# Two experts per token: rows of their own in memory in place of adding scatters into one row

## The chip, the cores and the metric

The kernel runs on one core of a Trainium2 chip. The metric is device time in microseconds (us), the median of several executions. A difference is called real here from 2% on.

## What is computed

The program is one layer of a decoder trunk for 512 tokens of width 1024. After a token mixer (state space, pooling, attention) with its residual comes a hierarchical mixture of 16 experts: each token picks one group of four experts and the two best experts in it, and their outputs are added to the residual with weights. A final norm ends it. Cut to what matters here:

```python
x = x + concat(A, B, C) @ w_out                 # x2 below: the residual of the second half
h = rms_norm(x, norm2_g)
# comb[t, e]: weight of expert e for token t; two of the 16 are not zero
act = silu(h @ w_gate[e]) * (h @ w_up[e]) * comb[:, e]
x = x + sum over e of act @ w_down[e]
out = rms_norm(x, final_norm_g)
```

## The kernel before

**Order of the work.** Streams of steps (Python generators such as `s_gate_up`, `s_down`, `y_out`, `s_meta`, `s_last`) are emitted in the order in which a planner (`Flow`) estimates that their engines would start them. A step names its engine, the events that it needs (`fl.sig`, `fl.sig_dma`) and the tokens that it takes. Each engine then runs its instructions in that fixed order and waits on semaphores. If an estimate changes, the order of everything behind it can change.

**Experts.** Each expert has 96 slots. The tokens' normed rows are scattered by GpSimd into `x_scr` (`scatter`), one slot for each of a token's two experts, and read back transposed as `xts`. The weights (fp32, 3 MB per expert) come through a ring of five staging buffers `stg` of 512 KB each. ScalarE writes the high fp16 half of each staged part, VectorE the low half (`gu`, `dn`), which frees the staging buffer. An expert is then 24 products for gate and up (`pg`), silu on ScalarE and a product on VectorE (`xs`), two transposes (`pta`), the split `aT`, and 12 products `py`. Experts overlap: TensorE does the products of one while the other engines finish the one before.

**Rows out (`y_out`).** VectorE scales the left half of an expert's 96 output rows into a buffer `ys`, ScalarE the right half. There are two such buffers. GpSimd then starts an indirect DMA that adds the rows to `acc_scr`, one row per token in device memory, which holds the residual x2 before (`s_acc`):

```python
pool.indirect_dma_start(
    out=acc_scr[:, :], out_offset=bass.IndirectOffsetOnAxis(ap=B["tok"][0:CAP, e:e + 1], axis=0),
    in_=ys[0:CAP, :], in_offset=None, compute_op=ALU.add)
```

All these DMAs write one tensor, and each waits for the one before. Unused slots point at spare rows behind the 512 tokens.

**The end.** The last expert (15) writes no rows to memory: TensorE multiplies its rows `ys` with a matrix of its tokens' places (`hot_e`) in `s_last`. Once the scatter of expert 14 has landed (`("y1", NE - 2)`), SP reads the four token tiles `xt` back from `acc_scr`. For tiles 0 and 1 VectorE adds the product to `xt`; for tiles 2 and 3 (`PADD`) TensorE adds `xt` by an fp32 product with the identity. Squares on ScalarE, a power on GpSimd and a scaling on VectorE end each tile, and SP stores it.

**Clears (`s_clear`).** SP writes zeros over `x_scr` (20 parts of 512 KB) and one part of `acc_scr` in the first quarter.

**Beyond the slots.** If an expert has more than 96 tokens, a dense pass at the end recomputes; it is behind a branch.

Of the kernel before, what the change touches and what calls it, by code (L numbers as in the profile page):

```python
# [9 lines left out]
F16 = mybir.dt.float16  # L10
# [9 lines left out]
P = 128  # L20
# [58 lines left out]
class _Engine:  # L79
    """An engine whose instructions also advance the flow's estimate of its time."""  # L80
# [16 lines left out]
class Flow:  # L97
    """Emits streams of instructions in the order in which their engines would start them.

    A stream is a generator. It yields (engine, needs, tokens) ahead of a step: the engine that the  # L100
    step starts on, events that other streams signal, and tokens to take. The step that could start
    first is emitted next; a lower rank goes first among equals.
    """
# [170 lines left out]
def hybrid_trunk_kernel(tc, a, out, cap=CAPACITY, dbg=None):  # L274
# [22 lines left out]
    m_scr = dram.tile([NSLOT + 2 * S, 2], F32, name="m_scr")  # L297
    acc_scr = dram.tile([S + P, D], F32, name="acc_scr")
# [9 lines left out]
    # Pages of 8 KB per partition, which change hands. Those of the experts' weights:  # L308
# [71 lines left out]
    def less_busy(margin):  # L380
        """Whether GpSimd is free so much earlier than VectorE."""
        return fl.free.get("dve", 0.0) > max(fl.t, fl.free.get("pool", 0.0)) + margin

# [28 lines left out]
    # weights of the dense layers and of the experts share one ring of staging buffers  # L412
# [140 lines left out]
    def s_prep():  # L553
# [26 lines left out]
        # (lambda_bar - 1) / lambda  # L580
# [28 lines left out]
    def s_prep_b():  # L609
        # chunk input map, transposed on the tensor engine  # L610
# [28 lines left out]
    def s_prep_e():  # L639
        # unit phases e^{i 8 theta c}, c = 0..63, and partners that invert them exactly  # L640
# [37 lines left out]
    def s_prep_c():  # L678
# [3 lines left out]
        # C lambda^tau, tau = 0..8 (imaginary part negated)  # L682
# [28 lines left out]
        # response within a chunk, laid out as a block Toeplitz matrix through DRAM  # L711
# [31 lines left out]
    def s_bias():  # L743
        # one row per query of a 64-query tile
# [31 lines left out]
    def s_clear():  # L776
        # rows of the routed tokens' buffer that no token takes read as zeros
        for r in range(0, NSLOT + 2 * S, P):
            yield "sp", ("zero", ("start", "k0"))
            sp.dma_start(x_scr[r:r + P, :].rearrange("p (j c) -> p j c", c=512),  # L780
                         zero.unsqueeze(1).to_broadcast([P, 4, 512]))
        yield "sp"
        sp.dma_start(acc_scr[S:S + P, :].rearrange("r (j c) -> r j c", c=256),
                     zero.bitcast(F32).unsqueeze(1).to_broadcast([P, 4, 256]))
        sp.dma_start(m_scr[0:NSLOT, :], a["meta0"])

# [415 lines left out]
    def s_norm2(m):  # L1202
        """x2 * norm2_g and its transpose for the router; 1 / rms comes in later."""
# [23 lines left out]
    pads = cst.tile([P, 4 * NT], F32, name="pads")  # L1227
    mt_ = cst.tile([P, NT, 2, 2], F32, name="mt_")
# [10 lines left out]
    def s_route(m):  # L1239
# [30 lines left out]
        # first of the largest groups, then the first two of its largest experts  # L1270
# [82 lines left out]
    def s_gather(m):  # L1353
        """The first expert's tokens, transposed: a product with the tokens' places, each part exact."""
# [21 lines left out]
    def s_gates():  # L1376
        """Gate weights, each with its token's number, and those of pairs beyond an expert's slots."""
# [6 lines left out]
        v.tensor_copy(mt_[:, :, :, 0], cpk[:, C_TOK:C_TOK + NT].unsqueeze(2).to_broadcast([P, NT, 2]))  # L1384
# [53 lines left out]
    def s_acc():  # L1438
        for m in range(NT):
            yield "sp", (("x2", m, 0), ("x2", m, 1))  # L1440
            sp.dma_start(acc_scr[m * P:(m + 1) * P, :], x2_t[m])
            fl.sig_dma(("acc", m))

# [1 line left out]
    we = {}  # L1445

    # When the places of the weights come free.
# [108 lines left out]
    def s_meta():  # L1556
        yield "pool", ("meta", "B")
        mt = B["ex"].tile([P, NE, 2], F32, tag="mt", name="mt", bufs=1)
# [8 lines left out]
        for t in range(NT):  # L1567
            yield "dve", (("dstart", 5),)
            if t == 0:
                B["hot"] = B["ex"].tile([P, S], F16, name="hot_e", bufs=1)  # L1570
            v.tensor_scalar(B["hot"][0:CAP, t * P:(t + 1) * P], cpk[0:CAP, C_COL:C_COL + P],
                            mt[0:CAP, NE - 1, 0:1], -float(t * P), ALU.subtract, ALU.is_equal)
# [5 lines left out]
        for t in range(NT):  # L1578
            yield "sp", (("y1", NE - 2),), ("stg",)
            xt[t] = stage.tile([P, D], F32, tag="stg", name=f"xt{t}")  # L1580
            sp.dma_start(xt[t], acc_scr[t * P:(t + 1) * P, :])
            fl.sig_dma(("xt", t))

    xt, yo = {}, {}
    PADD = (2, 3)               # tiles whose residual is added on TensorE
    ssz = cst.tile([P, NT, 3], F32, name="ssz")

    def s_last(ys):
        """The last expert's rows go to their tokens on TensorE, and the sum to SBUF."""
# [47 lines left out]

    def y_out(e, nh, py, ys):
# [19 lines left out]
        else:  # L1658
# [4 lines left out]
            pool.indirect_dma_start(  # L1663
                out=acc_scr[:, :], out_offset=bass.IndirectOffsetOnAxis(ap=B["tok"][0:CAP, e:e + 1], axis=0),
                in_=ys[0:CAP, :], in_offset=None, compute_op=ALU.add)
            fl.give("ys")
            fl.sig(("y1", e))

# [74 lines left out]
    rv = nc.values_load(flag[:1, :1], min_val=0, max_val=S)  # L1743
    with tc.If(rv > CAP):
        with tc.tile_pool(name="fb", bufs=1) as fb, tc.tile_pool(name="psF", bufs=2, space=PSUM) as psF:
            sp.dma_start(cov_scr, cov)
            gff = fb.tile([P, D], F32, name="gff")
            sp.dma_start(gff, a["final_norm_g"].to_broadcast([P, D]))
            xtf = [fb.tile([P, D], F32, name=f"xtf{t}") for t in range(NT)]
            for t in range(NT):  # L1750
                sp.dma_start(xtf[t], acc_scr[t * P:(t + 1) * P, :])
            hTf = fb.tile([P, KD, S], F32, name="hTf")
            hf = fb.tile([P, 2 * D], F16, name="hf")
            hs = fb.tile([P, D], F32, name="hs")
            for t in range(NT):
                pool.indirect_dma_start(
                    out=hf, out_offset=None, in_=x_scr[:, :],
                    in_offset=bass.IndirectOffsetOnAxis(ap=slot_i[:, t, 0:1], axis=0))
                v.tensor_tensor(hs, hf[:, 0:D], hf[:, D:], ALU.add)
                v.tensor_scalar(hs, hs, 1.0 / SA, None, ALU.mult)  # L1760
                for k in range(KD):
                    pt = psF.tile([P, 512], F32, tag="pf", name=f"pf{t}_{k}")
                    pe.transpose(pt[:, 0:P], hs[:, k * P:(k + 1) * P], ident)
                    v.tensor_copy(hTf[:, k, t * P:(t + 1) * P], pt[:, 0:P])
            wgf = fb.tile([P, 2, KD, FE], F32, name="wgf")
# [42 lines left out]
def layouts(i, cap=CAPACITY):  # L1808
    """The arrays of setup_inputs() as the kernel reads them, and constants of the shapes alone."""
# [51 lines left out]
    r["meta0"] = np.stack([S + np.arange(NE * cap) % cap, np.zeros(NE * cap)], axis=1).astype(np.float32)  # L1861
# [21 lines left out]
```

## Time and profile before

| | |
|---|---|
| median of 3 runs | 483.51 us |
| the runs | 477.53, 483.51, 498.87 us |
| span of the profiled execution | 482.8 us |
| time of that execution beyond its span | no other time is shown; the median lies 0.7 us above the span |
| busy share of the span | TensorE 81%, VectorE 62%, ScalarE 50%, GpSimd 32% |
| mean granted TensorE clock | 0.901 of full speed |

The span goes from the first to the last instruction. The shares are averages over stages with different limits: the mixers end at about 270 us, the experts fill 270 to 456 us, and the last norm ends the span. PE is TensorE, DVE VectorE, ACT ScalarE, POOL GpSimd, and SP the engine that issues most DMAs; PEld is TensorE's weight load.

### The profile page before, as it was taken

The numbers are of one execution on the slowest core, as the hardware profiler recorded it, in microseconds if no ns is written. First come the engines' busy times: TensorE is split into PE (matmuls) and PEld (weight loads), VectorE is DVE, ScalarE is ACT, GpSimd is POOL, SyncE is SP. The second block draws the span as 40 slices with busy tenths as digits, with TensorE's granted clock in tenths as the row PEclk, the third lists the DMA queues.
The fourth block names the chain that finished last, engine by engine and source line by source line (L and its number), as shares of the span: only waits on it lengthen the run. The fifth ranks groups of instructions, "written<-read, shape, count | busy, mean of one in ns | idle before, by whom it ended". The sixth has DMA issues, their size and how long they took to land. (4 is left out here: it accounts for less than half of the span.)

```text
span 482.8 us, 6649 instructions
## 1 busy us (share of the span) xinstructions
PE 389.6 (81%) x2344; PEld 222.2 (46%) x2344; DVE 301.0 (62%) x593; ACT 242.5 (50%) x399; POOL 155.7 (32%) x206
## 2 busy tenths in 40 slices
PE   2899777499979989999996828979979967867624
PEld 1697442354455556444564614545545533433211
DVE  2788609936647769864898952756667726445242
ACT  4742202435578948767756433645556525442222
POOL 1258982213110000104468580222111202256221
PEclk9999977799999999999996769898999995987857
DMA  8912559979984896822955579999999999863463
GB/s 282 302 46 46 73 95 312 380 247 325 175 224 149 280 303 229 294 86 97 335 188 220 201 169 253 296 265 342 267 307 308 362 151 335 247 208 71 63 230 132
DMA packets 70902, 107.35 MB, mean 222 GB/s; under 512 B 27891, under 2 KB 49811, under 8 KB 70868
## 3 DMA queue, kind: packets, MB, share of 16 engines
q1 hardware_dynamic: 67172, 96.55, 67.1%
q0 software_dynamic: 3136, 10.12, 9.4%
q10 hardware_dynamic: 560, 0.25, 0.3%
q8 instruction: 19, 0.31, 0.3%
q14 instruction: 15, 0.12, 0.1%
HBM read 74.14 MB, written 26.87 MB: 209 GB/s over the span
## 5 line engine op out<-in xcount | busy, mean ns | idle before, releaser
L89 PE MATMUL pg<-gu,xts 128*96 128x512 f16 x384 | 98.9, 406 | 6.2 <-DMA xts<-x_scr 6.2
L89 ACT ACTIVATE gu<-st_lde 128x1024 f16<-128x1024 f32 x64 | 66.7, 1053 | 51.2 <-DMA st_lde<-in_moe_w_up_dram 29.0
L89 DVE SCALAR_TENSOR_TENSOR gu<-st_lde,gu 128x1024 f16<-128x1024 f32 x61 | 73.8, 1219 | 27.1 <-ACT gu L89 27.0
L89 POOL DMA_INDIRECT acc_scr<-ys,tok x15 | 41.8, 2787 | 121.8 <-DMA acc_scr<-ys,tok 57.2
L89 PEld LDWEIGHTS <-xts 128*96 128x96 f16 x384 | 50.4, 133 | 44.2 <-issue 8.4
L89 PE MATMUL py<-dn,aT 128*96 128x512 f16 x192 | 50.1, 398 | 4.3 <-ACT aT L89 3.3
L89 DVE SCALAR_TENSOR_TENSOR dn<-st_lde,dn 128x1024 f16<-128x1024 f32 x32 | 39.9, 1255 | 15.2 <-ACT dn L89 15.2
L89 PE MATMUL px<-wo,cat 128*128 128x512 f16 x192 | 44.7, 379 | 0.0
L89 ACT ACTIVATE dn<-st_lde 128x1024 f16<-128x1024 f32 x32 | 33.2, 1050 | 16.0 <-DMA st_lde<-in_moe_w_down_dram 15.2
L89 PEld LDWEIGHTS <-aT 128*96 128x96 f16 x192 | 24.4, 130 | 25.6 <-ACT aT L89 3.9
L89 PEld LDWEIGHTS <-hT 128*64 128x64 f16 (+1 forms) x384 | 31.7, 157 | 7.3 <-issue 3.0
L89 DVE TENSOR_SCALAR ys<-py,cw 96x512 f32<-96x512 f32 x15 | 11.2, 745 | 37.6 <-DMA acc_scr<-ys,tok 25.8
L89 PE MATMUL ps_k<-hT,w_k 128*128 128x512 f16 x96 | 25.5, 424 | 5.0 <-ACT qk L89 5.0
L89 PE MATMUL pta<-cpk,xs 96*128 96x96 f32 x32 | 7.6, 323 | 25.9 <-DVE xs L89 25.8
L89 PEld LDWEIGHTS <-cat 128*128 128x128 f16 x192 | 18.2, 98 | 20.4 <-issue 2.4
L89 ACT ACTIVATE pr<-pr,nm 128x128 f32<-128x128 f32 (+3 forms) x32 | 17.9, 559 | 17.7 <-DVE nm L89 17.1
L89 PE MATMUL ps_v<-w_v,hT 128*128 128x256 f16 x192 | 25.8, 295 | 0.8 <-ACT hT L89 0.4
L89 POOL TENSOR_TENSOR gu<-st_lde,gu 128x1024 f16<-128x1024 f32 x3 | 7.0, 2349 | 59.7 <-ACT gu L89 59.7
L89 PE MATMUL psS<-qk 64*64 64x128 f32 (+3 forms) x128 | 24.9, 484 | 0.0
L89 PE MATMUL ps_q<-hT,w_q 128*128 128x512 f16 x96 | 22.5, 379 | 0.0
L89 ACT COPY pts<-ptp 128x128 f32<-128x128 f32 (+3 forms) x32 | 13.2, 422 | 17.4 <-PE ptp L89 17.2
L89 ACT ACTIVATE ys<-py,cw 96x512 f32<-96x512 f32 (+1 forms) x17 | 11.4, 676 | 20.0 <-DMA acc_scr<-ys,tok 17.1
(247 smaller groups left out, 651.8 us busy)
## 6 DMA issues: line engine op xcount, KB each, us to landing
st_lde<-in_moe_w_gate_dram SPq DMA_DIRECT2D x32, 512.0 KB, 6.6
st_lde<-in_moe_w_up_dram SPq DMA_DIRECT2D x32, 512.0 KB, 6.3
st_lde<-in_moe_w_down_dram SPq DMA_DIRECT2D x32, 512.0 KB, 6.8
x_scr<-zero SPq DMA_DIRECT2D x20, 512.0 KB, 6.4
xp<-in_x_dram SPq DMA_DIRECT2D x8, 512.0 KB, 10.0
st_ldo<-in_w_out_dram SPq DMA_DIRECT2D x6, 512.0 KB, 8.8
st_ld_v<-in_w_in_dram SPq DMA_DIRECT2D x4, 512.0 KB, 8.1
st_ld_q<-in_w_in_dram SPq DMA_DIRECT2D x4, 512.0 KB, 5.0
```

The lines of the kernel that those rows point to most:

```text
L89: r = f(*args, **kw)
```

## The change

Each of a token's two chosen experts gets a row of its own: the first choice row `token`, the second row `512 + token` of a new tensor `y_scr`. Unused slots get rows behind these. The scatters are plain writes; they are declared independent of each other. `x2_scr` holds the residual alone. At the end SP reads x2 (as `xt`, into the staging buffers, with no wait for the experts) and, after expert 14's rows have landed, both rows of each token (`yr`, 1 MB per tile), and `pair_sum` adds them on VectorE and GpSimd. The slot data `m_scr` carry a third number, the plain token, for `hot_e`. The planner counts a `ys` buffer as free, and `y1` as reached, when the scatter has landed, not when it is issued. Zeros go over 12 parts of `x_scr` and 8 of `y_scr`. The dense pass reads the new tensors.

```diff
-    m_scr = dram.tile([NSLOT + 2 * S, 2], F32, name="m_scr")
-    acc_scr = dram.tile([S + P, D], F32, name="acc_scr")
+    m_scr = dram.tile([NSLOT + 2 * S, 3], F32, name="m_scr")
+    x2_scr = dram.tile([S, D], F32, name="x2_scr")
+    y_scr = dram.tile([2 * S + NSLOT, D], F32, name="y_scr")
...
-        for r in range(0, NSLOT + 2 * S, P):
+        for r in range(0, NSLOT, P):
             yield "sp", ("zero", ("start", "k0"))
...
-        yield "sp"
-        sp.dma_start(acc_scr[S:S + P, :].rearrange("r (j c) -> r j c", c=256),
-                     zero.bitcast(F32).unsqueeze(1).to_broadcast([P, 4, 256]))
+        for r in range(0, 2 * S, P):
+            yield "sp"
+            sp.dma_start(y_scr[r:r + P, :].rearrange("r (j c) -> r j c", c=256),
+                         zero.bitcast(F32).unsqueeze(1).to_broadcast([P, 4, 256]))
...
+        v.tensor_copy(mt_[:, :, 0, 0], cpk[:, C_TOK:C_TOK + NT])
+        v.tensor_scalar(mt_[:, :, 1, 0], cpk[:, C_TOK:C_TOK + NT], float(S), None, ALU.add)
...
-            sp.dma_start(acc_scr[m * P:(m + 1) * P, :], x2_t[m])
+            sp.dma_start(x2_scr[m * P:(m + 1) * P, :], x2_t[m])
...
         for t in range(NT):
-            yield "sp", (("y1", NE - 2),), ("stg",)
+            yield "sp", (), ("stg",)
             xt[t] = stage.tile([P, D], F32, tag="stg", name=f"xt{t}")
-            sp.dma_start(xt[t], acc_scr[t * P:(t + 1) * P, :])
-            fl.sig_dma(("xt", t))
+            sp.dma_start(xt[t], x2_scr[t * P:(t + 1) * P, :])
+            fl.sig_dma(("x2r", t))
+        rows = y_scr[0:2 * S, :].rearrange("(i t p) d -> t p i d", i=2, t=NT)
+        for t in range(NT):
+            yield "sp", (("y1", NE - 2), ("dend", NE - 6))
+            yr[t] = page(YR[t], [P, 2, D], F32, f"yr{t}")
+            sp.dma_start(yr[t], rows[t])
+            fl.sig_dma(("yr", t))
+            fl.spawn(1, pair_sum(t))
+
+    def pair_sum(t):
+        eng, name = (pool, "pool") if t % 2 else (v, "dve")
+        yield name, (("yr", t), ("x2r", t))
+        eng.tensor_tensor(xt[t], xt[t], yr[t][:, 0], ALU.add)
+        yield "dve"
+        v.tensor_tensor(xt[t], xt[t], yr[t][:, 1], ALU.add)
+        fl.sig(("xt", t))
+
+    YR = ("p8", "p9", "p12", "p13")
...
             yield "pool"
-            pool.indirect_dma_start(
-                out=acc_scr[:, :], out_offset=bass.IndirectOffsetOnAxis(ap=B["tok"][0:CAP, e:e + 1], axis=0),
-                in_=ys[0:CAP, :], in_offset=None, compute_op=ALU.add)
-            fl.give("ys")
-            fl.sig(("y1", e))
+            pool.memset(pads[:, 4 * NT + e:4 * NT + e + 1], 0.0)
+            ins = pool.indirect_dma_start(
+                out=y_scr[:, :], out_offset=bass.IndirectOffsetOnAxis(ap=B["tok"][0:CAP, e:e + 1], axis=0),
+                in_=ys[0:CAP, :], in_offset=None)
+            for o_ in yscat:
+                tc.declare_no_dep(ins.ins, o_.ins, reason="rows are distinct")
+            yscat.append(ins)
+            fl.give_dma("ys")
+            fl.sig_dma(("y1", e))
...
-    r["meta0"] = np.stack([S + np.arange(NE * cap) % cap, np.zeros(NE * cap)], axis=1).astype(np.float32)
+    slot = np.arange(NE * cap)
+    r["meta0"] = np.stack([2 * S + slot, 0 * slot, 2 * S + 0 * slot], axis=1).astype(np.float32)
```

## Rows read from the trace of the kernel before

**Rows 1.** The table by stretches. Columns: stretch in us, its length, busy us and instructions of PE, PEld, DVE, ACT and POOL, granted clock, DMA share of the 16 engines, GB/s.

```profile
340.00:380.00 40.00, 37.09 (x174) 20.93 (x173) 27.19 (x36) 23.83 (x32) 6.18 (x4) 1.00 1.08 310
380.00:400.00 20.00, 14.57 (x67) 7.79 (x65) 8.86 (x10) 7.17 (x9) 4.27 (x2) 0.95 1.15 243
420.00:440.00 20.00, 11.14 (x41) 5.85 (x40) 10.03 (x12) 8.17 (x12) 10.03 (x2) 0.80 0.59 184
440.00:456.00 16.00, 11.95 (x49) 6.08 (x48) 5.21 (x9) 3.50 (x7) 6.44 (x3) 0.93 0.36 58
```

**Rows 2.** The tensor `acc_scr`: its adding scatters (duration on GpSimd in ns, minimum/median/maximum, first and last start), and who waited for a DMA into it (us in all, times).

```profile
L89 POOL DMA_INDIRECT acc_scr<-ys,tok x15: 1408/2113/7661, 305.7 to 455.1; - x15
...
  POOL acc_scr L89: 57.2, 7
  DVE ys L89: 25.8, 4
  ACT ys L89: 17.1, 4
```

**Rows 3.** GpSimd's timeline: the first and the last three of the 15 adding scatters (experts 0, 12, 13 and 14). Columns: start, duration, instruction, and in brackets the idle time before it and what ended it.

```profile
305.73 1.53 POOL L89 DMA_INDIRECT acc_scr<-ys,tok  x1 [12.81 <-ACT ys L89]
...
436.49 7.66 POOL L89 DMA_INDIRECT acc_scr<-ys,tok  x1 [7.51 <-DMA acc_scr<-ys,tok]
448.91 1.41 POOL L89 DMA_INDIRECT acc_scr<-ys,tok  x1 [4.76 <-DMA acc_scr<-ys,tok]
455.12 1.41 POOL L89 DMA_INDIRECT acc_scr<-ys,tok  x1 [4.79 <-DMA acc_scr<-ys,tok]
```

**Rows 4.** TensorE's timeline: the two transposes `pta` of experts 9, 10, 11, 13, 14 and 15, one pair for each expert.

```profile
377.87 0.48 PE L89 MATMUL pta<-cpk,xs 96*128 96x96 f32 x2
...
386.28 0.48 PE L89 MATMUL pta<-cpk,xs 96*128 96x96 f32 x2
...
401.87 0.60 PE L89 MATMUL pta<-cpk,xs 96*128 96x96 f32 x2 [7.15 <-DVE xs L89]
...
424.08 0.48 PE L89 MATMUL pta<-cpk,xs 96*128 96x96 f32 x2 [3.04 <-DVE xs L89]
...
438.12 0.59 PE L89 MATMUL pta<-cpk,xs 96*128 96x96 f32 x2 [5.82 <-DVE xs L89]
...
449.71 0.48 PE L89 MATMUL pta<-cpk,xs 96*128 96x96 f32 x2 [1.44 <-DVE xs L89]
```

**Rows 5.** VectorE's timeline from 397 us: rows `ys` of experts 10, 12 and 13, the product `xs` of experts 13 and 14, and the last expert's low halves.

```profile
397.96 0.75 DVE L89 TENSOR_SCALAR ys<-py,cw 96x512 f32<-96x512 f32 x1 [7.97 <-DMA acc_scr<-ys,tok]
...
421.81 0.75 DVE L89 TENSOR_SCALAR ys<-py,cw 96x512 f32<-96x512 f32 x1 [5.97 <-DMA acc_scr<-ys,tok]
...
423.61 0.41 DVE L89 SCALAR_TENSOR_TENSOR xs<-pg,xs 96x256 f32<-96x256 f32 x1
...
435.85 0.75 DVE L89 TENSOR_SCALAR ys<-py,cw 96x512 f32<-96x512 f32 x1 [8.16 <-DMA acc_scr<-ys,tok]
...
437.64 0.41 DVE L89 SCALAR_TENSOR_TENSOR xs<-pg,xs 96x256 f32<-96x256 f32 x1
...
455.17 1.40 DVE L89 SCALAR_TENSOR_TENSOR ys<-py,cw,ys 96x512 f16<-96x512 f32 x2 [4.22 <-ACT ys L89]
```

**Rows 6.** ScalarE's timeline: a split of expert 13's up weights, expert 13's silu, and the last expert's high halves.

```profile
399.17 1.06 ACT L89 ACTIVATE gu<-st_lde 128x1024 f16<-128x1024 f32 x1 [7.46 <-DMA st_lde<-in_moe_w_up_dram]
...
418.06 0.38 ACT L89 ACTIVATE xs<-pg 96x256 f32<-96x256 f32 x1 [2.53 <-PE pg L89]
...
454.45 1.26 ACT L89 ACTIVATE ys<-py,cw 96x512 f16<-96x512 f32 x2 [3.90 <-DMA acc_scr<-ys,tok]
```

**Rows 7.** VectorE's groups by line from 300 to 456 us: the low halves of the weights, the scaled rows, the product and the split of one expert (shape, count, busy us, mean ns, idle time before).

```profile
L89 DVE SCALAR_TENSOR_TENSOR gu<-st_lde,gu 128x1024 f16<-128x1024 f32 x36 | 43.6, 1218 | 12.6 <-ACT gu L89 12.5
...
L89 DVE TENSOR_SCALAR ys<-py,cw 96x512 f32<-96x512 f32 x15 | 11.2, 745 | 37.6 <-DMA acc_scr<-ys,tok 25.8 <-PE py L89 6.4 <-PE pg L89 5.4
L89 DVE SCALAR_TENSOR_TENSOR xs<-pg,xs 96x256 f32<-96x256 f32 x15 | 6.2, 415 | 2.3 <-ACT xs L89 2.3
L89 DVE SCALAR_TENSOR_TENSOR aT<-pta,aT 128x192 f16<-128x192 f32 x15 | 5.2, 349 | 0.9 <-ACT aT L89 0.9
```

**Rows 8.** DMA: GpSimd's queue q0 from 340 to 390 us (adding scatters), the same queue from 257 to 283 us (plain scatters of 4 KB rows to `x_scr`, and small ones), with packets, MB and share of the 16 engines; then the issues of both kinds over the whole run, with the median us from issue to landing.

```profile
q0 software_dynamic: 548, 1.92, 19.7%
...
q0 software_dynamic: 1097, 3.67, 36.2%
...
acc_scr<-ys,tok POOLq DMA_INDIRECT x15, 10.6
...
x_scr<-xp,slot_i POOLq DMA_INDIRECT x6, 5.0
```

**Rows 9.** The timeline of the end: SP reads the four tiles, VectorE adds to tile 0, TensorE starts the residual of tile 2, and its last product ends at 475.66 us. The last line, from the page's groups, is GpSimd's price for a two-input operation of 128x1024.

```profile
460.42 1.75 SPq L89 DMA_DIRECT2D xt<-acc_scr  x4
...
463.84 1.29 DVE L89 TENSOR_TENSOR xt<-pf,xt 128x512 f32<-128x512 f32 x2 [7.27 <-DMA xt<-acc_scr]
...
467.63 2.04 PE L89 MATMUL pf<-xt,cpk 128*128 128x512 f32 x2 [8.52 <-DMA xt<-acc_scr]
...
475.06 0.60 PE L89 MATMUL pf<-ys,hot_e 96*128 96x512 f16 x2
...
L89 POOL TENSOR_TENSOR gu<-st_lde,gu 128x1024 f16<-128x1024 f32 x3 | 7.0, 2349 | 59.7 <-ACT gu L89 59.7
```

More of the change, by code (lines that the diff above doesn't have):

```diff
@@ L1226, in hybrid_trunk_kernel @@
     F_ = {}
-    pads = cst.tile([P, 4 * NT], F32, name="pads")
-    mt_ = cst.tile([P, NT, 2, 2], F32, name="mt_")
+    pads = cst.tile([P, 4 * NT + NE], F32, name="pads")
+    mt_ = cst.tile([P, NT, 2, 3], F32, name="mt_")
     def scatter(m, dst, src, i):
@@ L1383, in s_gates @@
         v.tensor_tensor(ge[:, :, 4:5], m8[:, :, 1:2], m8[:, :, 0:1], ALU.subtract)
-        v.tensor_copy(mt_[:, :, :, 0], cpk[:, C_TOK:C_TOK + NT].unsqueeze(2).to_broadcast([P, NT, 2]))
+        v.tensor_copy(mt_[:, :, :, 2], cpk[:, C_TOK:C_TOK + NT].unsqueeze(2).to_broadcast([P, NT, 2]))
+        v.tensor_copy(mt_[:, :, 0, 0], cpk[:, C_TOK:C_TOK + NT])
+        v.tensor_scalar(mt_[:, :, 1, 0], cpk[:, C_TOK:C_TOK + NT], float(S), None, ALU.add)
         yield "act"
@@ L1557, in s_meta @@
         yield "pool", ("meta", "B")
-        mt = B["ex"].tile([P, NE, 2], F32, tag="mt", name="mt", bufs=1)
+        mt = B["ex"].tile([P, NE, 3], F32, tag="mt", name="mt", bufs=1)
         pool.dma_start(mt[0:CAP], m_scr[0:NSLOT, :].rearrange("(e c) w -> c e w", c=CAP))
@@ L1571, in s_meta @@
             v.tensor_scalar(B["hot"][0:CAP, t * P:(t + 1) * P], cpk[0:CAP, C_COL:C_COL + P],
-                            mt[0:CAP, NE - 1, 0:1], -float(t * P), ALU.subtract, ALU.is_equal)
+                            mt[0:CAP, NE - 1, 2:3], -float(t * P), ALU.subtract, ALU.is_equal)
         fl.sig("hot_e")
@@ L1578, in s_meta @@
         for t in range(NT):
-            yield "sp", (("y1", NE - 2),), ("stg",)
+            yield "sp", (), ("stg",)
             xt[t] = stage.tile([P, D], F32, tag="stg", name=f"xt{t}")
-            sp.dma_start(xt[t], acc_scr[t * P:(t + 1) * P, :])
-            fl.sig_dma(("xt", t))
-    xt, yo = {}, {}
+            sp.dma_start(xt[t], x2_scr[t * P:(t + 1) * P, :])
[14 more added lines that the diff above has]
+        fl.sig(("xt", t))
+    xt, yr, yo = {}, {}, {}
+    YR = ("p8", "p9", "p12", "p13")
     PADD = (2, 3)
@@ L1636, in last_scale @@
             sp.dma_start(out[t * P:(t + 1) * P, :], y)
+    yscat = []
     def y_out(e, nh, py, ys):
@@ L1748, in hybrid_trunk_kernel @@
             sp.dma_start(gff, a["final_norm_g"].to_broadcast([P, D]))
+            g2f = fb.tile([P, D], F32, name="g2f")
+            sp.dma_start(g2f, a["norm2_g"].to_broadcast([P, D]))
             xtf = [fb.tile([P, D], F32, name=f"xtf{t}") for t in range(NT)]
-            for t in range(NT):
-                sp.dma_start(xtf[t], acc_scr[t * P:(t + 1) * P, :])
             hTf = fb.tile([P, KD, S], F32, name="hTf")
-            hf = fb.tile([P, 2 * D], F16, name="hf")
             hs = fb.tile([P, D], F32, name="hs")
             for t in range(NT):
[L1756 to L1760, printed above, removed]
+                sp.dma_start(xtf[t], x2_scr[t * P:(t + 1) * P, :])
+                rs = rstd(fb, xtf[t], f"h{t}", hs.bitcast(F16)[:, 0:D])
+                v.scalar_tensor_tensor(hs, xtf[t], rs, g2f, ALU.mult, ALU.mult)
                 for k in range(KD):
                     pt = psF.tile([P, 512], F32, tag="pf", name=f"pf{t}_{k}")
-                    pe.transpose(pt[:, 0:P], hs[:, k * P:(k + 1) * P], ident)
+                    pe.transpose(pt[:, 0:P], hs.rearrange("p (c k) -> p k c", k=KD)[:, k], ident)
                     v.tensor_copy(hTf[:, k, t * P:(t + 1) * P], pt[:, 0:P])
+            for t in range(NT):
+                for i in range(2):
+                    yf = fb.tile([P, D], F32, tag="yf", name=f"yf{t}_{i}")
+                    sp.dma_start(yf, y_scr[i * S + t * P:i * S + (t + 1) * P, :])
+                    v.tensor_tensor(xtf[t], xtf[t], yf, ALU.add)
             wgf = fb.tile([P, 2, KD, FE], F32, name="wgf")
```

## The prediction, made before the changed kernel was run

> **What bounds the kernel now.** I read the table by stretches first, to see where the span goes [rows 1]. From 340 to 380 us TensorE is busy 37.1 of 40 us and the DMA engines are full (share 1.08). From 420 to 440 us TensorE is busy 11.1 of 20 us, at a mean granted clock of 0.80 (part of the time on the lower of its two levels), and the DMA share falls to 0.59, then to 0.36. So the first part of the experts is well fed, and in the last part neither TensorE nor the transfers are full: something waits.
>
> The tensor view of `acc_scr` says for what [rows 2]. GpSimd waited 57.2 us in seven adding scatters for the scatter before, VectorE 25.8 us and ScalarE 17.1 us for a scatter to land before they could write `ys` again. GpSimd's timeline shows the chain [rows 3]: 15 scatters from 305.73 to 455.12 us, one every 149.39 / 14 = 10.67 us, and the median from issue to landing is 10.6 us [rows 8]. That is a serial chain running at its own latency.
>
> Next, the pace of the experts, read from the transposes `pta` on TensorE [rows 4]. Experts 9 to 10 are 386.28 - 377.87 = 8.4 us apart, experts 10 to 15 on average (449.71 - 386.28) / 5 = 12.7 us. Every late `pta` waited for VectorE's `xs`. On VectorE `xs` stands in its queue behind a `ys` that waits for a scatter [rows 5]: 7.97, 5.97 and 8.16 us for experts 10, 12 and 13. Expert 13's silu was done at 418.06 + 0.38 = 418.4 us [rows 6], and its `xs` began at 423.61. Between them VectorE sat behind `ys` until 421.81. The chain of waits reaches the products that way: scatter, `ys`, VectorE's queue, `xs`, TensorE.
>
> One place is less clear. At expert 11 ScalarE waited for weights until 399.17 us [rows 6], later than the `ys` wait on VectorE, which ended at 397.96. Without the scatters that wait for the weights would still have been there.
>
> **The change, part by part.** All sums are made against the profiled execution, span 482.8 us. The median of the runs lies 0.7 us above it, which I add at the end.
>
> *Plain writes in place of adds.* From 340 to 390 us the scatter queue held 19.7% of 16 engines over 50 us, 157.6 us, for 1.92 MB, 469 rows of 4 KB: 336 ns a row. Plain scatters to `x_scr` held 36.2% over 26 us, 150.6 us, for 896 rows: 168 ns [rows 8]. An expert's 96 rows fall from 96 x 336 / 16 = 2.0 us of all engines to 1.0 us. Thirteen of these lie ahead of the last weights, 13 us of DMA time. While the DMA engines are full that makes weights come earlier. What it is worth on TensorE by itself from 340 to 380 us is at most the 2.9 us in which TensorE is idle there [rows 1], and at least nothing; I take 1.5.
>
> *No wait between scatters, `ys` free sooner.* This is the main term. A plain scatter lands about 5.0 us after issue [rows 8], its buffer is wanted two experts later, some 16.8 us at 8.4, less the time to fill it. So the `ys` waits should go. What is then next? VectorE: an expert costs it six weight halves at 1.218, and 0.745 + 0.415 + 0.349 for `ys`, `xs`, `aT` [rows 7], 8.8 us together, against 8.4 for TensorE. Experts 10 to 15 took 63.4 us. At VectorE's pace they would take 44.1, a gain of 19.3; at TensorE's 42.1, a gain of 21.4. If expert 11's excess of 15.6 - 8.8 = 6.8 us stays, because there the weights were late too, the gain is 12.5. Eight scatters have by then given 8 us of DMA time back, which speaks for the weights coming in time, but the DMA engines were at 1.15 there [rows 1]; I take half of the 6.8 and get 15.9, bounds 12.5 and 21.4. The granted clock should come back with the steadier work; I count nothing extra.
>
> *Expert 15's rows.* ScalarE waited 3.90 us for a scatter before it could write them [rows 6]. The last products run during part of that wait, so the gain is between 0 and 3.9; I take 1.8.
>
> *The end.* Expert 15's rows are ready at 455.17 + 1.40 = 456.6 us [rows 5], and the span ends 26.2 us later. The read of the tiles is issued at 460.42, since the last scatter starts only at 455.12, behind its predecessor [rows 3]. After the change expert 14's scatter starts when its rows are ready, one pace of 8.4 us ahead of expert 15's, and lands 5.0 us later: 3.4 us ahead of them. If writing its descriptors takes 7.66 us on GpSimd as at 436.49 and not 1.41 [rows 3], it lands 2.9 us behind them. Then the reads: tile 0 was used 3.4 us after issue, tile 2 after 7.2, so 1.9 us for each 0.5 MB [rows 9]. Tiles of 1 MB make 5.3 + 3 x 3.8 = 16.7 us until the fourth; by the plain packets, 256 x 168 / 16 = 2.7 us per MB, it is 12.8. Tile 3 needs a GpSimd add of 2.35 us [rows 9] and a VectorE add, for which I take the 1.22 us of a weight half of the same size [rows 7]: 3.6. TensorE took 475.66 - 467.63 = 8.0 us for tiles 2 and 3, so 4.0 for one, and 7.1 us follow its last product [rows 9]. Together 27.5 to 31.4 us from the issue of the reads, in place of 22.4. Measured from expert 15's rows the end is 24.1 to 34.3 us away, against 26.2. I take reads that need 14 us, issued 2 us ahead: 26.7, a loss of 0.5, bounds from a gain of 2.1 to a loss of 8.1. The other adds of `pair_sum` (five on VectorE, one on GpSimd) hide under these reads; uncovered they would cost 1.2 or 2.35 us each. The reads of x2 lie under expert 15, when the DMA share is 0.36 [rows 1]. They wait for staging buffers, and only the reads of `yr` and the stores are behind them on SP.
>
> *Small edits.* One clear fewer on SP, a third column in `m_scr`, a GpSimd memset ahead of each scatter, two short VectorE operations for the slot data: nothing, since none is at an engine that this chain waits for; with no cover, under 1.5 us either way, inside the bounds above.
>
> **Sum.** 15.9 + 1.5 + 1.8 - 0.5 = 18.7 us. 482.8 - 18.7 = 464.1, with 0.7 about 465 us. All best ends (21.4 + 2.9 + 3.9 + 2.1 = 30.3) give 453, all worst (12.5 - 8.1 = 4.4) give 479.
>
> **Rivals.**
>
> *The wait for weights takes the place of the wait for scatters* (as at expert 11). For it: DMA shares over 1 until 400 us. Against it: 0.59 and 0.36 after, where most of the `ys` waits lie, and 13 us given back. If the late stages win only half of 12.5 us, with 1.8 at expert 15 and 3 lost in the reads, the time is 483.5 - 5 = 478.5 us.
>
> *Scatters get slow beside VectorE.* The scatter at 436.49 us took 7.66 us on GpSimd, the ones at 448.91 and 455.12, with VectorE idle before them, 1.41 each [rows 3]. VectorE's weight halves have two inputs from on-chip memory, and without its waits it has fewer gaps. Up to 7.66 + 5.0 = 12.7 us to landing this stays inside the two experts' pace of 16.8 us, so it decides only at the last scatter: 6.2 us more, about 471 us. The Trainium skill (SBUF — State Buffer, section Who interferes with whom) says that a VectorE instruction with two on-chip inputs contends with a GpSimd instruction that reads that memory, though it infers that the writing of descriptors is not held up by such operations; the row at 436.49 speaks for a hold-up. By the first part the sum would be the 471 of this rival, by the inference the 465 of the forecast.
>
> *The planner's new order undoes the overlap on TensorE.* The planner now counts `ys` as taken until its estimate of the landing, which stands behind all loads in its own DMA queue. From an estimate of more than two paces (16.8 us) on, it puts an expert's `py` behind further products, or has no other work to put between `xs`, `pta` and `py`. Where no other work stood ahead of it, `pta` cost TensorE 1.44 to 3.04 us of idle time [rows 4]. Fourteen experts at 2.2 us are 31 us, less the 19 of the forecast: 12 us lost, 495 us. Against it: loads in flight are limited to three parts, a few us at the 310 GB/s of [rows 1].
>
> *The scatters stay in a chain*, because some other dependence holds them together. Then only the adds' 1.0 us per link is saved; the late links still decide, and about 7 of them save 7 us: 476 us.
>
> **How the numbers follow.** Forecast 0.62; slow scatters 0.15; weights 0.12; chain stays 0.05; planner's order 0.06. The first two are faster by over 2% (below 473.8 us), which is about what a measurement of this kernel can tell from no change. The next two are within 2%, the last is slower (above 493.2 us). A little of the forecast's worst end lies within 2%, and a little of the weights' case beyond: faster 0.77, same 0.17, slower 0.06. The range from 453 to 479 holds all but the planner's case and the tails.
>
> **What would show it.** In the changed kernel's trace the scatters should start within about 2 us of their `ys` and overlap in flight, GpSimd's and VectorE's waits for them should be near zero, experts 10 to 15 should be 8.4 to 9.5 us apart, with the granted clock near 1.0, and a row of the scatter queue should cost near 168 ns. Expert 15's rows should be ready near 437 us. The reads `yr` should be issued within 3 us of that, and the end should follow 24 to 34 us after. The forecast is wrong if VectorE's or ScalarE's wait for `st_lde` grows by what the wait for scatters loses, if `pta` waits for something new, or if the end takes more than 34 us.

## The result and the profile after

The changed kernel takes 456.0 us (median of four runs, 452.28 to 460.38), the kernel before 480.52 beside it: a ratio of 0.950, 95% interval 0.939 to 0.962. The profiled execution took 456.77 us with a span of 455.0, so 27.8 us less span than before. Runs of the kernel before spread widely, from 463 to 501 us over the chips of this study, and nothing here explains that spread; the variants below are therefore compared by the stages of one profiled execution each, with each median beside them. A difference of two or three us in one stage is no more than single executions differ by: the four runs of the changed kernel alone lie 8 us apart from the fastest to the slowest.

The stretches of the changed kernel (columns as in [rows 1]; busy TensorE is the first number behind the length, then come the weight loads, VectorE, ScalarE and GpSimd):

```profile
340.00:380.00 40.00, 38.00 (x178) 21.57 (x177) 29.15 (x34) 25.92 (x35) 6.07 (x10) 1.00 1.09 330
380.00:400.00 20.00, 18.44 (x86) 10.21 (x85) 14.06 (x16) 10.84 (x15) 2.49 (x4) 1.00 1.04 321
400.00:420.00 20.00, 17.92 (x83) 9.84 (x81) 12.54 (x15) 11.48 (x17) 3.24 (x5) 1.00 0.99 368
420.00:440.00 20.00, 6.91 (x23) 2.81 (x24) 14.03 (x15) 4.44 (x11) 10.10 (x8) 0.66 0.54 215
```

From 380 to 420 us TensorE is now busy 36.4 of 40 us at the full clock. The hole of [rows 1] at 420 to 440, in the middle of the experts, is gone; the low stretch that remains there is the end. Where from 380 to 400 us 243 GB/s moved at a DMA share of 1.15, 321 move at 1.04: the scatter queue there takes 11.2% of the engines' time for 0.90 MB, in place of 18.0% for 0.46 MB.

The view of the tensor `y_scr`, which answers to [rows 2], and the scatter queue from 340 to 390 us, which answers to [rows 8]:

```profile
L89 POOL DMA_INDIRECT y_scr<-ys,tok x15: 911/970/4121, 301.0 to 416.2; - x15
...
its engine sat idle before it (us, times) until:
  ACT ys L89: 82.7, 12
```
```profile
q0 software_dynamic: 582, 2.06, 10.2%
```

Among the experts no engine waits for a scatter any more: GpSimd waits for ScalarE's half of `ys`, that is, for work. The median issue costs 0.97 us in place of 2.11. The queue holds 10.2% of 16 engines over 50 us, 81.6 us for 2.06 MB or 503 rows: 162 ns a row, half of what a row cost before.

The transposes `pta` of experts 10 to 15 on TensorE (as [rows 4]):

```profile
376.24 0.48 PE L89 MATMUL pta<-cpk,xs 96*128 96x96 f32 x2 [0.78 <-DVE xs L89]
384.34 0.37 PE L89 MATMUL pta<-cpk,xs 96*128 96x96 f32 x2
392.78 0.48 PE L89 MATMUL pta<-cpk,xs 96*128 96x96 f32 x2 [0.31 <-DVE xs L89]
402.53 0.36 PE L89 MATMUL pta<-cpk,xs 96*128 96x96 f32 x2
408.82 0.48 PE L89 MATMUL pta<-cpk,xs 96*128 96x96 f32 x2
419.34 0.48 PE L89 MATMUL pta<-cpk,xs 96*128 96x96 f32 x2 [0.93 <-DVE xs L89]
```

They are 8.1, 8.4, 9.8, 6.3 and 10.5 us apart, 43.1 together against 63.4 before. Expert 11's step fell from 15.6 to 8.1.

The end, read from the timelines of SP, VectorE, GpSimd and TensorE (start, duration, engine, operation, and idle time before it with what ended it), which answers to [rows 9]:

```profile
421.80 2.10 SPq L89 DMA_DIRECT2D yr<-y_scr  x4
...
423.79 0.75 DVE L89 SCALAR_TENSOR_TENSOR ys<-py,cw,ys 96x512 f16<-96x512 f32 x1 [0.50 <-ACT ys L89]
426.58 2.49 DVE L89 TENSOR_TENSOR xt<-xt,yr 128x1024 f32<-128x1024 f32 x2 [2.04 <-DMA yr<-y_scr]
...
434.62 2.33 POOL L89 TENSOR_TENSOR xt<-xt,yr 128x1024 f32<-128x1024 f32 x1
435.04 2.99 DVE L89 TENSOR_TENSOR xt<-xt,yr 128x1024 f32<-128x1024 f32 x1
...
438.09 2.07 PE L89 MATMUL pf<-xt,cpk 128*128 128x512 f32 x2 [12.27 <-DVE xt L89]
...
447.96 1.41 DVE L89 SCALAR_TENSOR_TENSOR yo<-pf,ssz,gf 128x512 f32<-128x512 f32 x2 [1.18 <-POOL ssz L89]
```

Expert 15's rows are ready at 423.79 + 0.75 = 424.5 us and the span ends 30.5 us later, 26.2 before: the one stage that got longer.

The whole span in five stages, in us, for the two kernels and the variants of the next section (first `pg` of expert 0; from there to expert 1's `pta`; `pta` of expert 1 to `pta` of expert 15; from there to expert 15's rows; from there to the end):

| kernel | to first `pg` | to expert 1 | 1 to 15 | to rows | end | span | median |
|---|---|---|---|---|---|---|---|
| before | 273.1 | 29.7 | 147.0 | 6.9 | 26.2 | 482.8 | 480.5 |
| changed | 268.1 | 26.7 | 124.6 | 5.2 | 30.5 | 455.0 | 456.0 |
| A plain, chained | 269.3 | 27.7 | 122.3 | 5.2 | 32.0 | 456.4 | 455.8 |
| B adds, unchained | 269.0 | 27.3 | 132.9 | 5.2 | 32.1 | 466.5 | 467.5 |
| C before, three `ys` | 279.1 | 27.2 | 135.0 | 5.2 | 25.2 | 471.7 | 473.0 |
| D before, one clear fewer | 268.6 | 29.4 | 142.1 | 6.7 | 26.2 | 473.0 | 475.3 |
| E changed, one clear more | 274.1 | 28.6 | 123.3 | 5.2 | 29.9 | 461.1 | 462.6 |
| F before, C and D | 271.1 | 28.5 | 134.1 | 5.2 | 25.1 | 463.9 | 464.8 |
| G one row read | 266.4 | 27.9 | 123.3 | 5.2 | 22.3 | 445.1 | 450.4 |
| H identity for tiles 0, 1 | 268.6 | 28.7 | 123.2 | 5.2 | 28.8 | 454.4 | 456.5 |
| I no identity | 267.9 | 26.9 | 128.9 | 5.2 | 28.0 | 456.8 | 455.9 |
| J sums on VectorE | 266.1 | 28.1 | 121.7 | 5.2 | 28.6 | 449.7 | 457.4 |
| K J and I | 267.6 | 28.7 | 124.9 | 5.2 | 28.4 | 454.8 | 455.3 |
| L J, two by product | 269.1 | 29.0 | 125.2 | 7.8 | 26.7 | 457.9 | 456.7 |

### The profile page after: what moved, and what is told of

It is laid out like the page before. It is cut to its first block, busy times and chain, and to the rows that moved or that the text cites. A ratio compares the mean times of both kernels' runs of the same rounds, so it can differ in the third digit from the quotient of the medians.

```text
span 455.0 us, 6678 instructions
## 1 busy us (share of the span) xinstructions
PE 377.5 (83%) x2344; PEld 218.2 (48%) x2344; DVE 314.0 (69%) x604; ACT 239.8 (53%) x396; POOL 135.2 (30%) x220
## 5 line engine op out<-in xcount | busy, mean ns | idle before, releaser
L89 PE MATMUL pg<-gu,xts 128*96 128x512 f16 x384 | 93.7, 389 | 10.5 <-DMA xts<-x_scr 9.6
L89 DVE SCALAR_TENSOR_TENSOR gu<-st_lde,gu 128x1024 f16<-128x1024 f32 x63 | 76.2, 1220 | 23.4 <-ACT gu L89 23.4
L89 ACT ACTIVATE gu<-st_lde 128x1024 f16<-128x1024 f32 x64 | 66.5, 1052 | 36.4 <-DMA st_lde<-in_moe_w_gate_dram 18.3
L89 PEld LDWEIGHTS <-xts 128*96 128x96 f16 x384 | 48.3, 128 | 45.8 <-DMA xts<-x_scr 10.0
L89 PE MATMUL py<-dn,aT 128*96 128x512 f16 x192 | 47.5, 383 | 4.2 <-ACT aT L89 3.4
L89 POOL DMA_INDIRECT y_scr<-ys,tok x15 | 18.6, 1242 | 106.1 <-ACT ys L89 82.7
L89 ACT ACTIVATE dn<-st_lde 128x1024 f16<-128x1024 f32 x32 | 33.2, 1052 | 14.2 <-DMA st_lde<-in_moe_w_down_dram 13.3
L89 ACT ACTIVATE pr<-pr,nm 128x128 f32<-128x128 f32 (+3 forms) x32 | 17.8, 557 | 24.9 <-DVE nm L89 24.5
L89 PE MATMUL ps_k<-hT,w_k 128*128 128x512 f16 x96 | 24.1, 408 | 5.6 <-ACT qk L89 5.6
L89 POOL TENSOR_TENSOR xg<-xp,g 128x512 f32<-128x512 f32 x4 | 5.9, 1486 | 58.5 <-PE po L89 58.3
L89 PE MATMUL ptp<-cpk,pr 128*128 128x128 f32 x80 | 14.7, 288 | 9.8 <-DVE rcp L89 7.9
L89 ACT COPY pts<-ptp 128x128 f32<-128x128 f32 (+3 forms) x32 | 13.2, 420 | 12.2 <-PE ptp L89 12.1
L89 PEld LDWEIGHTS <-w_k 128*128 128x128 f16 x96 | 9.5, 103 | 18.7 <-issue 9.6
L89 PEld LDWEIGHTS ptp<-cpk,pr 128*128 128x128 f32 x80 | 9.4, 143 | 18.4 <-issue 13.9
```

The lines of the kernel that those rows point to most:

```text
L89: r = f(*args, **kw)
```

## The experiments

Kernels of one group ran on one chip: A to D (the kernel before: 487.4 us there), E and G to I (493.0), F, J and K (491.9), L alone (494.6). Against the kernel before on their own chip, A gains 31.6 us, B 19.9, C 14.4, D 12.1 and F 27.1.

**A. Plain scatters that wait for each other.**

```diff
-            for o_ in yscat:
-                tc.declare_no_dep(ins.ins, o_.ins, reason="rows are distinct")
-            yscat.append(ins)
```

> The changed kernel, but its plain scatters wait for each other again. If the independence of the scatters brought the gain, the chain of 15 is back and the time is 468 us or more, with GpSimd waiting for y_scr in front of most scatters. If the low latency of a plain scatter brought it (median 7.8 us from issue to landing in the changed kernel, under the 8.6 us pace of its experts), a chain of them keeps up and the time is 456 to 460 us.

455.8 us, the same as the changed kernel: the second expectation holds. From the view of `y_scr`, GpSimd's idle time ahead of its scatters that a landing ended:

```profile
  DMA y_scr<-ys,tok: 15.3, 2
```

Two waits on GpSimd, 15.3 us in all; VectorE's waits came to 0.6. So the declared independence is worth nothing here. A plain scatter lands in 6.6 us at the median, under the pace of 122.3 / 14 = 8.7, and this chain, whose links are shorter than the pace, holds VectorE up by no more than that.

**B. Independent scatters that add.**

```diff
-                in_=ys[0:CAP, :], in_offset=None)
+                in_=ys[0:CAP, :], in_offset=None, compute_op=ALU.add)
```

> The changed kernel, but each scatter adds onto its cleared row instead of writing it, and the scatters stay independent. If the removed waits brought the gain, only the DMA time comes back (about 1 us per scatter while the engines are full): 457 to 464 us, with packets near 330 ns in the scatter queue. If the cheaper packets brought it, most of the 24 us is lost: 470 us or more.

467.5 us, 11.5 behind the changed kernel and between the two expectations, although no `ys` waits for a landing. The scatter queue from 340 to 390 us, and ScalarE's waits for the three kinds of weights over the whole span, of B and then of the changed kernel:

```profile
q0 software_dynamic: 580, 2.05, 20.7%
...
  DMA st_lde<-in_moe_w_gate_dram: 21.2, 15
  DMA st_lde<-in_moe_w_down_dram: 19.7, 16
  DMA st_lde<-in_moe_w_up_dram: 18.4, 16
```
```profile
  DMA st_lde<-in_moe_w_gate_dram: 18.3, 12
  DMA st_lde<-in_moe_w_up_dram: 16.4, 16
  DMA st_lde<-in_moe_w_down_dram: 13.3, 10
```

As many packets hold the engines twice as long, 20.7 against 10.2% (331 ns a row against 162), and the waits for weights are 59.3 us against 48.0. In experts 1 to 15 alone (296.26 to 429.18 and 294.71 to 419.34 us) they are 41.7 against 33.3: 8.4 us more, where that stage is 8.3 us longer, 132.9 against 124.6. The eight other kernels here with plain scatters stand at 121.7 to 128.9 in it, so the 8.3 is uncertain by some 4 us either way, but B stands above them all. The other 3.2 us of span lie in the stages around it, where single executions differ as much. The table by stretches gives the DMA engines a share of 0.96 over experts 1 to 15 in the kernel before, and 1.07 in C, 1.06 here and 1.05 in the changed kernel: once no `ys` waits for a scatter, the DMA engines are full throughout, and then the adds' time on them counts.

**C. The kernel before with three `ys` buffers.** The adds stay, in their chain.

```diff
-        ys = ex_p.tile([P, D], F32, tag="ys", name=f"ys{e}")
+        ys = ex_p.tile([P, D], F32, tag="ys", name=f"ys{e}", bufs=3)
...
-        for k_, n in (("pg", 2), ("pta", 2), ("py", 4), ("ex", 2), ("ys", 2)):
+        for k_, n in (("pg", 2), ("pta", 2), ("py", 4), ("ex", 2), ("ys", 3)):
```

> The kernel before, with three buffers ys in place of two; the adding scatters stay in their chain. If the waits for ys were what held the products up, VectorE and ScalarE wait less for scatters, the experts come closer together from expert 10 on, and the time falls by 8 us or more. If the chain's own length (15 links of 10.7 us) sets the end, the last scatter lands near 460 us as before and the time stays within 1% of 480 us.

473.0 us, as the first expectation has it. No `ys` waits for a landing any more. Experts 10 to 15 take 51.4 us in place of 63.4, expert 11's step still 16.1. The scatters of C on GpSimd:

```profile
L89 POOL DMA_INDIRECT acc_scr<-ys,tok x15: 1410/1422/2956, 310.2 to 445.3; - x15
```

The slow issue of 7.66 us in [rows 3] is gone as well. It belongs to the same wait: VectorE's `ys` and GpSimd's next scatter wait for one landing, so the scatter starts as VectorE begins the work that had piled up (`ys` at 435.85 in [rows 5], the scatter at 436.49 in [rows 3]), and a slow issue lands later still. D, which keeps two buffers, shows the same long issues, 6.52 and 7.66 us; F, with three, at most 2.89. So read, the steps of 11 to 14 us at the end of [rows 4] are the `ys` wait feeding itself; without it the chain of adds keeps pace.

**D. The kernel before with one clear fewer.**

```diff
-        for r in range(0, NSLOT + 2 * S, P):
+        for r in range(0, NSLOT + 2 * S - P, P):
```

> The kernel before, with 19 in place of 20 clears of x_scr (the last 128 spare rows are not cleared). Only the planner's estimate of the DMA time after the clears moves. If the 5 us by which the changed kernel reached the first expert sooner (268.1 against 273.1 us) came from the new order that one clear fewer gives, the first expert's products start near 268 us here, and the time is 473 to 477 us. If they were the scatter of single executions, the start stays near 273 us and the time at 480 us, within 1%.

475.3 us, as the first expectation has it, with expert 0's first product at 268.64 us instead of 273.05; most of the rest of the 9.8 us of span lies in experts 1 to 15. That the changed kernel clears 20 parts where the kernel before cleared 21 was put at nothing in the prediction.

**E. The changed kernel with one clear more.**

```diff
-        for r in range(0, 2 * S, P):
+        for r in range(0, 2 * S + P, P):
```

> The changed kernel, with nine in place of eight clears of y_scr, so 21 clears as before the change. If the order that one clear fewer gives brought the 5 us ahead of the first expert, its products start near 273 us again and the time is 459 to 463 us. If not, it starts near 268 us and the time stays at 456 us within 1%.

462.6 us, first product at 274.09: the first expectation again. The 6.6 us against the changed kernel are 1.4% of the time, less than is called real here; the start of the first product says more. Over all kernels here: with 20 parts to clear (eleven kernels) it lies at 266.1 to 271.1 us, with 21 parts (before, E, C) at 273.1, 274.1 and 279.1. The order of the instructions on TensorE, VectorE and ScalarE differs from about 120 us on between D and the kernel before, though one DMA of 512 KB is all that was taken out; the changed kernel and E part at the same place, where with 20 parts ScalarE and VectorE split a part of the attention's key weights earlier. Between 4.4 us (D) and 6.0 us (E) at the first product go with it. Which of the moved instructions they come from was not looked for, and no run keeps the order and takes out the transfer alone.

**F. The kernel before with C and D together.**

> The kernel before (adds in a chain, two reads of nothing new at the end) with one clear fewer and with three ys buffers together. If the order after one clear fewer (5 us) and the waits for ys (10 to 12 us) are separate parts of the gain, they add up: 466 to 469 us, first products of expert 0 near 268.5, experts 10 to 15 about 50 us, expert 11's step still 14 us or more. What then is left to the changed kernel (about 11 us, less the 4 us that its end lost) is the adds' DMA time. Rival, that the two act on the same wait: 471 to 474 us.

464.8 us, a little under the 466 to 469 expected: the two parts nearly add up, 9.8 and 11.1 us of span alone, 18.9 together (in the medians 12.1 and 14.4, and 27.1). The first product is at 271.1 us, not near 268.5, and experts 10 to 15 take 44.4, not 50. With the adds, their chain and the old end all kept, 18.9 of the change's 27.8 us are there already. Experts 1 to 15 take 134.1 us, near B's 132.9, and 9.5 more than in the changed kernel; by B most of that is the adds' DMA time. Expert 11's long step stands in another place, 14.0 us to expert 10 and 11.0 to expert 11; B has 8.8 and 9.0 there.

**G. One row of the two is read and added.** The second row of each token, and so a part of the result, is left out.

```diff
-            sp.dma_start(yr[t], rows[t])
+            sp.dma_start(yr[t][:, 0], rows[t][:, 0])
...
-        yield "dve"
-        v.tensor_tensor(xt[t], xt[t], yr[t][:, 1], ALU.add)
```

> The changed kernel without the read and the add of each token's second row at the end (that part of the result is left out): 2 MB in place of 4 MB, one add per tile. It prices the added reads and adds. By my working (1.3 to 1.9 us per 0.5 MB, one VectorE add of 1.2 us per tile) the end comes 6 to 9 us sooner: 447 to 450 us. If the reads hide under other work, 453 us or more.

450.4 us, near the 447 to 450 expected, the end 22.3 us: the second rows' 2 MB and four adds cost 8.1 us of the end in the profiled runs and 5.6 in the medians. VectorE's first adds of G:

```profile
423.04 1.23 DVE L89 TENSOR_TENSOR xt<-xt,yr 128x1024 f32<-128x1024 f32 x1 [0.27 <-DMA yr<-y_scr]
...
425.81 2.00 DVE L89 TENSOR_TENSOR xt<-xt,yr 128x1024 f32<-128x1024 f32 x1
```

It starts 0.3 us after expert 15's rows, not 2.0.

**H and I. Which tiles TensorE adds.** H adds the sums of tiles 0 and 1 by the identity in place of 2 and 3 (and gives their PSUM buffers back after use), I those of none.

```diff
-    PADD = (2, 3)
+    PADD = (0, 1)
...
+        if t in PADD:
+            fl.give("py")
```
```diff
-    PADD = (2, 3)
+    PADD = ()
```

> The changed kernel, with the residual of tiles 0 and 1 in place of 2 and 3 added by the identity product on TensorE. In the changed kernel the end takes 30.5 us from expert 15's rows (424.5 to 455.0 us), and TensorE stands idle from 425.8 to 438.1 us until tile 2 is summed, then needs 8.1 us. If that late start of TensorE sets the end, TensorE now starts near 430 us and the time falls by 3 to 5 us, to 451 to 453. If the reads of yr and the adds on VectorE set it, the time stays within 1.5 us of 456.

> The changed kernel, with no identity product: VectorE adds TensorE's sums to all four tiles (two more operations of 0.65 us for each of tiles 2 and 3). If TensorE's late 8.1 us set the end, the time falls by 3 to 6 us, to 450 to 453. If VectorE's queue sets it, the added 2.6 us on VectorE show and the time is 456 to 459.

456.5 and 455.9 us, ends of 28.8 and 28.0. TensorE's 12.27 us of waiting for tile 2 looks like the bound of the end and isn't by itself: 1.7 and 2.4 us of the end go in the profiled runs, and the times stay, as the second expectation of each has it.

**J. All sums on VectorE.**

```diff
-        eng, name = (pool, "pool") if t % 2 else (v, "dve")
+        eng, name = v, "dve"
```

> The changed kernel, with all eight adds of the rows on VectorE and none on GpSimd. Theory that GpSimd's adds and the order behind them lengthen the end (they take 2.3 us each, they start late behind the powers, and a VectorE add beside one takes 3.0 instead of 1.2 us): the fourth tile's sum is ready about 3 us earlier, the end from expert 15's rows takes 27 to 28 us instead of 30.5, time 452 to 454 us. Rival, that the reads of the rows alone set the pace of the tiles: no change, 455 to 457 us. Rival, that VectorE becomes the bound of the end with 2.4 us more work: 458 us.

457.4 us at the median, though the profiled run, at 451.5, was the fastest of its six. VectorE's adds in J:

```profile
427.08 3.61 DVE L89 TENSOR_TENSOR xt<-xt,yr 128x1024 f32<-128x1024 f32 x3
...
431.81 2.35 DVE L89 TENSOR_TENSOR xt<-xt,yr 128x1024 f32<-128x1024 f32 x2
```

Every add takes 1.2 us here; beside GpSimd's add it took 2.99 in the changed kernel and 2.00 in G. The end is 28.6 us, 1.9 shorter, but the expected gain in time did not come; the stages of J are those of its fastest run.

**K. J without the identity.**

```diff
-        eng, name = (pool, "pool") if t % 2 else (v, "dve")
+        eng, name = v, "dve"
...
-    PADD = (2, 3)
+    PADD = ()
```

> As the kernel with all adds of the rows on VectorE, and without the products with the identity: VectorE adds the last expert's product to all four tiles. If VectorE is far from being the bound of the end: 451 to 454 us, the end 26 to 28 us. If it becomes the bound (20.3 us of adds and scalings from the first read on, 426.6 + 20.3 + 5.6): 452.5 us at best, and 1 to 2 us later than the kernel with the identity.

455.3 us. VectorE's first and last rows of the end:

```profile
428.44 2.48 DVE L89 TENSOR_TENSOR xt<-xt,yr 128x1024 f32<-128x1024 f32 x2 [2.03 <-DMA yr<-y_scr]
...
443.42 4.71 DVE L89 SCALAR_TENSOR_TENSOR yo<-xt,ssz,gf 128x512 f32<-128x512 f32 x7
```

It works from 428.44 to 448.13 us without a wait in between, and the span ends 6.7 us later: here VectorE is the bound of the end.

**L. J, and expert 14's rows kept on the chip too.** TensorE multiplies them with a matrix of their own, and the reads wait for expert 13's scatter.

```diff
-            yield "sp", (("y1", NE - 2), ("dend", NE - 6))
+            yield "sp", (("y1", NE - 3), ("dend", NE - 6))
...
-        if e == NE - 1:
+        if e >= NE - 2:
```

> As the kernel with all adds of the rows on VectorE, and expert 14's rows stay on the chip as well: TensorE multiplies them with a matrix of their tokens' places, as it does for expert 15, so the reads of the rows wait for expert 13's scatter only. If the issue of the reads behind the last scatter is what stretches the end: the reads are issued some 6 us earlier, near 415, VectorE does not wait for them, and the end from expert 15's rows takes 24 to 26 us in place of 28.6, time 451 to 454 us. Rival, that VectorE's own work in the end (17 to 18 us of adds and scalings in one row) and the last store (6 us) set it: 27 to 28 us and 454 to 456 us.

456.7 us, no gain, and neither expectation describes it. The issue of the reads, the first add, and the table by stretches of L:

```profile
421.02 2.43 SPq L89 DMA_DIRECT2D yr<-y_scr  x4
...
429.30 1.23 DVE L89 TENSOR_TENSOR xt<-xt,yr 128x1024 f32<-128x1024 f32 x1 [1.99 <-DMA yr<-y_scr]
...
412.00:421.00 9.00, 8.11 (x39) 4.37 (x38) 6.79 (x9) 5.82 (x9) 0.91 (x1) 1.00 0.95 373
421.00:433.00 12.00, 7.99 (x33) 3.71 (x32) 5.22 (x7) 2.08 (x4) 0.00 (x0) 0.90 0.97 376
```

The experts of this run stood 4.0 us later than in the changed kernel (`pta` of expert 15 at 423.37). Against them the reads are earlier, 2.3 us ahead of that `pta` instead of 2.5 behind it. But the first tile now takes 8.3 us to arrive, not 4.8: the DMA engines are full (0.95, then 0.97) with the last weights, x2's reads and then the rows, until 433 us. The add for tile 0 also stands between the two halves of expert 15's rows on VectorE, and delays the second by 2.6 us. Of the versions that compute the whole result, none beats the changed kernel by more than these runs can tell.

## Why the prediction was right

Forecast 465 us, measured 456.0, inside 453 to 479. The gain was 24.5 us from the median beside it, forecast 18.5. In span it was 27.8 us, forecast 18.7: experts 1 to 15 gave 5.0 more than forecast, the end lost 3.7 more, and 8.0 came from two stretches at which I had put nothing. That the first two nearly cancel is luck.

- **The main term held, its parts were other than I thought.** Experts 10 to 15 gained 20.3 us (forecast 15.9, bounds 12.5 and 21.4), experts 1 to 10 gained 2.0 (forecast 1.5). Taken as one stretch, experts 1 to 15 go from 147.0 to 135.0 without the `ys` waits (C), to 132.9 without the chain (B) and to 124.6 without the adding (changed): 12.0 us for the `ys` waits (8.0 between D and F, which differ in the third buffer alone), near my lower bound of 12.5; 2.1 between C and B, for the chain and all else in which these two differ, which is no more than single executions differ by; 8.3 for the adds' time on the DMA engines. That the scatters would overlap in flight was not needed, and they hardly do: a landing takes 7.8 us at the median, where I had 5.0, against steps of 124.6 / 14 = 8.9.
- **That last term was mis-sized.** I had given it 1.5 us, from TensorE's idle time between 340 and 380 us, and half of expert 11's excess of 6.8, 4.9 together. By the prices of a row (331 and 162 ns) the adds of 14 experts hold all engines 14 x 96 x 169 / 16 = 14.2 us longer, an estimate; 8.3 of that reached the time. B pays the 8.3 mostly in experts 1 to 10 (88.1 us against 81.5), the kernel before and C at expert 11 (15.6 and 16.1). I take these for one debt, weights that come late because of the adds: the sums agree and the place changes. What fixes the place was not isolated.
- **Small edits were not free.** One clear fewer was put at 0, at most 1.5 us either way. It moved the planner's order, and expert 0's first product came 5.0 us earlier; D and E show as much, 4.4 and 6.0, in either direction. This is the step that failed: an edit on an engine that nobody waits for was held to be free. With the 5.0 the sum would have been 23.7 and the forecast 460.
- **From the first product to expert 1** the changed kernel gained 3.0 us that no term held. A to L stand at 26.9 to 29.4 there, so it is mostly the spread of single runs; it stays open.
- **Expert 15's rows** came 1.7 us sooner after `pta`, forecast 1.8: ScalarE's wait of [rows 6] is gone.
- **The end lost 4.2 us**, forecast 0.5, bounds from a gain of 2.1 to a loss of 8.1. The issue was as worked out: reads 2.7 us ahead of expert 15's rows, against 2 assumed. The reads themselves were quicker than my 14 us: the last is issued by 423.2 and lands 10.9 later, 12.4 after the first issue. The adds that were to hide under them did not all: the first waits for its tile until 426.58, GpSimd's for tile 3 starts at 434.62, behind the powers of tile 0 and half a us after its rows landed, and the second add of tile 2 takes 2.99 us beside it. So TensorE starts tile 2 only at 438.09, 16.3 us after the first issue, and both of its tiles stand behind that, 8.1 us, where I had counted 4.0 for one; from its last product to the end it is 8.9 us, not 7.1. These are the terms of the end that were too small. G puts a price on the added half: 6 to 8 us. H to L show that no one of the rest sets the end: take away TensorE's share, GpSimd's, or the late issue, and the next in the row is VectorE or the transfers.

Of what was to show it, the waits, the price of a row (162 ns for 168), the clock, the reads within 3 us and the end within 24 to 34 came as written; experts 10 to 15 are 8.6 us apart on the mean, with single steps from 6.3 to 10.5. Two signs did not: the scatters hardly overlap, and expert 15's rows were ready at 424.5 us and not near 437.

Of the rivals, the wait for weights did not grow (48.0 us; the same view of the kernel before sums to 64.6). The scatters stayed quick but for one, the second, here with VectorE's two lines beside it:

```profile
306.50 4.12 POOL L89 DMA_INDIRECT y_scr<-ys,tok  x1 [4.38 <-ACT ys L89]
...
304.95 3.48 DVE L89 SCALAR_TENSOR_TENSOR gu<-st_lde,gu 128x1024 f16<-128x1024 f32 x3
...
308.62 1.21 DVE L89 SCALAR_TENSOR_TENSOR dn<-st_lde,dn 128x1024 f16<-128x1024 f32 x1
```

It ends at 310.62, 0.79 us after VectorE's last weight half of that run. That is no exception. Seven of the changed kernel's 15 scatters take longer than 0.97 us (1.06 to 4.12), and each of the seven ends 0.79 us after the end of one of VectorE's weight halves; the two that ran with VectorE idle took 0.91. In the kernel before the nine that took longer than 1.53 us end 1.28 to 1.34 us after one, that of 436.49 as well. So the hold-up that this rival feared is there; it stays small because six of the seven waited for one half only, the scatter above for three, and at the last scatter VectorE was idle. The Trainium skill (SBUF — State Buffer, section Who interferes with whom) says that a VectorE instruction with two on-chip inputs contends with a GpSimd instruction that reads that memory; the adds of 2.99 us beside 1.2 alone agree. It infers that the writing of descriptors is not held up by a `tensor_tensor`; these weight halves are another operation with two on-chip inputs, and beside them the scatters are held up. Whether it is the writing of descriptors that waits, or the reading of the row numbers `tok`, no run here separates.

The planner's order undid nothing among the experts, and the chain, as A shows, would have cost nothing had it stayed: that rival was priced at 476 us and measures 455.8.

## What to carry to other kernels

Compare a serial chain's link with the pace of its users before you break the chain: a shorter link or one more buffer may do, and a wait that makes two engines start at once can lengthen the next link. Where the DMA engines are full, take an accumulating transfer's extra packet time as the upper bound of its price (14.2 us here, of which 8.3 showed), not the idle time of the engine that it feeds (2.9). Where a planner writes the order from estimates, do not take an edit ahead of a stage to be free: measure it alone, in both directions.

## What the runs showed of the hardware that was not expected

A VectorE add of 128 x 1024 took 2.99 us beside GpSimd's add of the same size, which kept its own 2.33, and 1.2 us alone. It ends 1.08 us after GpSimd's (434.62 + 2.33 and 435.04 + 2.99); in G it takes 2.00 us and again ends 1.08 after GpSimd's, which runs from 424.38 for 2.35. Read so, VectorE waits for the other to end and then takes about its usual time. The GpSimd scatter of 96 rows without the add costs 0.91 us to issue undisturbed, 1.41 with it (C). And the long issues, up to 7.66 us, went away with a third buffer alone (2.96 at most in C), the adding kept: the longer issues end 0.79 us (plain, changed kernel) or about 1.3 us (adding, kernel before) after one of VectorE's weight halves, so their length goes with VectorE's run of work when they start, and not with the adding alone.
